# Decoder step on one core: conditioning blocks loaded ahead of x, the first 40 output tiles computed before the root, and TensorE held to program order

## The chip, the core and the metric

One core of a Trainium2 chip runs the whole program. TensorE (PE, with its weight loads PEld) multiplies into PSUM, VectorE (DVE) and ScalarE (ACT) read and write PSUM and SBUF, GpSimd (POOL) works on SBUF, and SyncE (SP) issues the DMAs. The time is that of one execution in device microseconds; several executions are made and their median is the number that counts.

## What is computed

A decoder layer for 256 prompt tokens and 8 x 4 sample tokens (288 columns in all), with model width 2048. What bears on the change is its beginning:

```python
mod = (jax.nn.silu(c) @ w_ada + b_ada).reshape(n, N_MOD, 1, D_MODEL)
sh_m, sc_m, gt_m, sh_f, sc_f, gt_f = [mod[:, i] for i in range(N_MOD)]
h = _rms(x, g_mix) * (1 + sc_m) + sh_m      # _rms: x * rsqrt(mean(x*x) + eps) * gain
proj = h @ w_in                             # 2048 -> 9216
```

After it come a gated convolution, a spatial gating, two projections, a residual, a second modulated norm, a SwiGLU layer of 5632 and a final norm. The conditioning `c` has nine rows: one for the prompt, eight for the sample groups.

## The kernel before

Everything is kept transposed: 128 features on the partitions, 288 tokens along the free axis, so `x` is 16 tiles (kt 0 to 15) of 128x288. `proj` has 72 output tiles. Every fp32 product is made of three fp32r matmuls: ACT rounds the weights to `hi` (line 331) and DVE makes `lo` = weights - `hi` (line 333), 512 columns at a time, and the activations are split in the same way; lines 344 to 346 then issue hi x hi, hi x lo, lo x hi.

Weights come in blocks of up to 1 MB through one ring of five `raw` buffers, all issued by SP in the order of a list of steps; a block is loaded five blocks ahead (`AHEAD`), when the block that had its buffer is done with. `proj` is accumulated in four passes over the input features: wA takes kt 0 for all 72 tiles (six blocks of 12 tiles) and stores each tile to `part[m]` (`sinkA`: ACT copies odd tiles, line 434, DVE even ones, line 436); wB adds kt 1 and 2 (nine blocks of eight tiles, `sinkB`, line 439), wC kt 3 to 7 (24 blocks of three), wD kt 8 to 15. Between them the conditioning blocks run on TensorE (`Ada`, line 274): aA gives the shift and scale of kt 0, aB of kt 1 and 2, aC and aD of kt 3 to 7, aE of 8 to 15. An `Ada` unit ends with `tail`: ACT copies the sums out (line 289), TensorE gathers or transposes them (293, 298), DVE adds the bias (302).

The order at the start: SP issues c, the first constants, all of x (2.4 MB), the other constants and then the four aA blocks. ACT squares x tile by tile, DVE adds the squares up, six small matmuls (167) and a power on POOL (171) give the root per token (`rstd1`), `norm1` spreads it over the partitions (177) into `rb1`, and `normed` x tiles are multiplied by it: kt 0 on DVE (197), the fifteen others on POOL (`norm1b`, 410). `mk_h1` makes the modulated activations h1 by ACT (205), POOL (208, 209), ACT (211) and DVE (216). Only then can the first wA matmul run.

The program is scheduled by a planner that orders each engine's instructions by a model of their costs; `issue_after(i)` tells it to place an instruction behind i on its engine. Each engine then works through its own queue strictly in that order, waiting on semaphores.

Of the kernel before, what the change touches and what calls it, by code (L numbers as in the profile page):

```python
# [15 lines left out]
NB = 8  # L16
# [6 lines left out]
SPB = 4  # L23
GK = 0.7978845608028654
# [21 lines left out]
    "wA": (0, 1, 12),  # L46
# [31 lines left out]
def _body(tc, nc, d, pc, pw, pslot, ptmp, pps):  # L78
# [35 lines left out]
    ident = cp[:, C_ID : C_ID + 128]  # L114
# [13 lines left out]
    V.memset(ones, 1.0)  # L128
    mhalf = const("mhalf", [P, 3])
# [70 lines left out]
    def modulate(ks, get, gm, sh0, out):  # L200
        hs, his = {}, {}

        def affine(k, t):
# [5 lines left out]
            G.tensor_tensor(sam(h[:, TP:]), sam(h[:, TP:]), bc4(mod[:, sh0 + k, 1:]), ALU.add)  # L209
# [34 lines left out]
    class Step:  # L244
        defer = False
        raw = None
        parts = None

    class Ada(Step):
# [15 lines left out]
        def run(self):  # L265
# [4 lines left out]
            for k in range(self.nk // ks):  # L270
                for j in range(4):
                    kt = self.blk * self.nk + k * ks + j % ks
                    o = (k * 4 + j) * w
                    self.last = PE.matmul(  # L274
                        acc[32 * j : 32 * j + 32, :w],
                        cs[:, kt, :],
                        self.raw[:, o : o + w],
                        start=(kt < ks),
                        stop=(kt >= 16 - ks),
                        tile_position=(0, 32 * j),  # L280
                        skip_group_check=True,
                    )
# [26 lines left out]
    class Blk(Step):  # L309
        def __init__(self, name, idx, rhs, sink):  # L310
            self.name, self.idx, self.rhs, self.sink = name, idx, rhs, sink
# [7 lines left out]
        def split(self, most=99):  # L319
# [4 lines left out]
            for s in range(len(self.parts), n, per):  # L324
# [6 lines left out]
                A.copy(hi, self.raw[:, s * 128 : e * 128])  # L331
# [5 lines left out]
        def run(self):  # L337
            for j in range(self.nm):
                ps = psmain()
                for k in range(self.nk):  # L340
# [3 lines left out]
                    PE.matmul(ps[:, :T], wh, ah, start=first, stop=False)  # L344
                    PE.matmul(ps[:, :T], wh, al, start=False, stop=False)  # L345
                    PE.matmul(ps[:, :T], wl, ah, start=False, stop=last)  # L346
                self.sink(self.idx * self.nm + j, ps)

    class KBlk(Blk):
        def run(self):  # L350
# [3 lines left out]
            for k in range(self.nk):  # L354
                ah, al = self.rhs(self.idx * self.nk + k)
                first, last = self.idx + k == 0, self.idx == nb - 1 and k == self.nk - 1
                for j in range(self.nm):
                    ps = S["kps"][j]
                    wh, wl = self.parts[k * self.nm + j]
                    PE.matmul(ps[:, :TU], wh, ah, start=first, stop=False)  # L360
                    PE.matmul(ps[:, :TU], wh, al, start=False, stop=False)
                    self.last = PE.matmul(ps[:, :TU], wl, ah, start=False, stop=last)
# [49 lines left out]
    xn = {}  # L412
    h1 = {}

    def mk_h1(k0, k1):
        def f():
            V.scalar_tensor_tensor(  # L417
                gm1[:, k0:k1, :],
                mod[:, 16 + k0 : 16 + k1, :],
                1.0,  # L420
# [430 lines left out]
```

## Time and profile before

| | us |
|---|---|
| median of three runs | 1659.89 (1659.48 to 1660.59) |
| the profiled execution, its own time | 1658.19 |
| its span on the core | 1656.2 |
| TensorE busy, share of the span | 1624.6, 98% |
| first matmul of wA starts at | 23.42 |

The profiled execution is 1.7 us under the median, and its span lies 2.0 us inside its own time. Times below count from the start of the span. A matmul's row lasts until its result has landed, so rows of matmuls overlap; their pace is read from how many start in a stretch.

### The profile page before, as it was taken

Reading aid. Unit: us, or ns where it says so; the run is one execution under the profiler, and the core shown is the slowest. Engines: PE = TensorE matmul, PEld = TensorE weight load, DVE = VectorE, ACT = ScalarE, POOL = GpSimd, SP = SyncE. Lnnn points to the kernel's source line nnn. Section 1 sums busy time; section 2 is a strip of 40 time slices with the busy share of each in tenths; the row PEclk is TensorE's granted clock in tenths of the full one; section 3 lists DMA queues with packets and bytes.
Section 4 is the critical chain, followed back from the end, with each engine's and each line's share of the span. In section 5 each row is a group of like instructions: output and inputs, shape, how many; then the busy total and the mean of one; then the engine's idle time right before and its main releaser. Section 6 shows DMA issues by size and latency. Waiting matters only on the chain.

```text
span 1656.2 us, 31141 instructions
## 1 busy us (share of the span) xinstructions
PE 1624.6 (98%) x12456; PEld 1556.0 (94%) x12456; DVE 995.4 (60%) x2034; ACT 736.2 (44%) x1371; POOL 63.9 (4%) x154
## 2 busy tenths in 40 slices
PE   5999999999999999999999999999999999999997
PEld 5889899989898999999999899999999999999997
DVE  5767556878755557557844455555555555555565
ACT  4534334643444434446733344444444444344453
POOL 3000001000000000002300000000000000000000
PEclk9999999999999999999999999999999999999998
DMA  7685786567777776674466755443454444645342
GB/s 267 254 335 207 277 313 246 191 233 261 277 308 277 282 286 251 251 263 154 152 255 254 304 170 196 171 163 137 158 206 163 168 141 156 204 161 171 126 170 76
DMA packets 56034, 357.59 MB, mean 216 GB/s; under 512 B 6369, under 2 KB 8577, under 8 KB 22737
## 3 DMA queue, kind: packets, MB, share of 16 engines
q1 hardware_dynamic: 55536, 354.88, 58.8%
q8 instruction: 97, 1.59, 0.4%
q0 software_dynamic: 352, 0.73, 0.1%
q14 instruction: 49, 0.39, 0.1%
HBM read 352.50 MB, written 3.09 MB: 215 GB/s over the span
## 4 chain that ended last, share of the span: by engine, by line
issue 50%; DVE 0%; ACT 0%; POOL 0%; PE 0%; POOLq 0%; DVEq 0%
DVE x L651 0%; PE px L177 0%; ACT t L205 0%; ACT s L211 0%; POOL t L208 0%; ACT hi L331 0%; POOL t L209 0%; POOLq L837 0%; DVE s L197 0%; DVE s L216 0%; DVEq L837 0%; POOLq L208 0%
## 5 line engine op out<-in xcount | busy, mean ns | idle before, releaser
L344 PE MATMUL pm<-s,hi 128*128 128x288 f32 x3712 | 1100.1, 297 | 7.2 <-ACT s L434 3.1
L345 PE MATMUL pm<-s,hi 128*128 128x288 f32 x3712 | 1097.1, 296 | 0.1
L346 PE MATMUL pm<-s,lo 128*128 128x288 f32 x3712 | 1094.1, 295 | 0.0
L331 ACT CAST hi<-raw 128x512 fp32r<-128x512 f32 (+1 forms) x966 | 581.9, 610 | 793.0 <-PE pm L345 661.7
L333 DVE TENSOR_TENSOR lo<-raw,hi 128x512 fp32r<-128x512 f32 (+1 forms) x966 | 652.5, 682 | 450.7 <-ACT hi L331 434.7
L344 PEld LDWEIGHTS pm<-s,hi 128*128 128x128 f32 x3712 | 698.8, 188 | 26.7 <-issue 14.6
L346 PEld LDWEIGHTS pm<-s,lo 128*128 128x128 f32 x3712 | 699.2, 188 | 0.2 <-DVE lo L333 0.2
L345 PEld LDWEIGHTS pm<-s,hi 128*128 128x128 f32 x3712 | 698.8, 188 | 0.5 <-DVE s L216 0.5
L274 PE MATMUL ada<-raw,cs 128*32 128x512 f32 (+2 forms) x960 | 91.1, 519 | 12.3 <-DMA raw<-in_aA 12.2
L439 DVE TENSOR_TENSOR s<-pm,s 128x288 f32<-128x288 f32 x144 | 64.3, 454 | 48.4 <-PE pm L346 48.2
L274 PEld LDWEIGHTS ada<-raw,cs 128*32 128x32 f32 x960 | 29.0, 113 | 56.4 <-issue 39.0
L447 DVE TENSOR_TENSOR s<-pm,s 128x288 f32<-128x288 f32 x72 | 32.8, 455 | 24.1 <-PE pm L346 23.8
L190 ACT CAST s<-t 128x288 fp32r<-128x288 f32 (+1 forms) x76 | 32.9, 432 | 21.0 <-DVE t L550 9.6
L192 DVE TENSOR_TENSOR s<-t,s 128x288 fp32r<-128x288 f32 (+1 forms) x76 | 34.8, 458 | 7.1 <-ACT s L190 7.0
L171 POOL TENSOR_TENSOR r<-r,mhalf 128x3 f32<-128x3 f32 x4 | 3.8, 957 | 908.2 <-DVE r L170 908.2
L232 DVE SCALAR_TENSOR_TENSOR x<-pm,mod,x 128x256 f32<-128x256 f32 x80 | 37.9, 474 | 0.0
L623 DVE SCALAR_TENSOR_TENSOR t<-t,pm 128x288 f32<-128x288 f32 x42 | 19.1, 454 | 25.3 <-PE pm L346 25.3
L231 DVE TENSOR_TENSOR t<-pm,mod 128x32 f32<-128x32 f32 x80 | 15.3, 191 | 29.6 <-PE pm L346 29.6
L155 DVE TENSOR_TENSOR acc<-acc,t 128x288 f32<-128x288 f32 x48 | 21.9, 456 | 12.3 <-ACT t L150 11.0
L150 ACT ACTIVATE t<-x 128x288 f32<-128x288 f32 x45 | 19.1, 442 | 21.3 <-DVE x L233 20.6
L457 ACT ACTIVATE s<-s 128x288 f32<-128x288 f32 x32 | 14.2, 445 | 14.2 <-DVE s L447 14.1
L208 POOL TENSOR_TENSOR t<-s,gm 128x32 f32<-128x32 f32 x32 | 11.3, 357 | 235.7 <-DVE gm L417 219.1
(114 smaller groups left out, 494.5 us busy)
## 6 DMA issues: line engine op xcount, KB each, us to landing
raw<-in_fi SPq DMA_DIRECT2D x84, 1024.0 KB, 4.8
raw<-in_a SPq DMA_DIRECT2D x64, 1024.0 KB, 6.4
raw<-in_f SPq DMA_DIRECT2D x64, 704.0 KB, 4.1
raw<-in_wD SPq DMA_DIRECT2D x36, 1024.0 KB, 6.3
raw<-in_wC SPq DMA_DIRECT2D x24, 960.0 KB, 6.2
raw<-in_aE SPq DMA_DIRECT2D x16, 1024.0 KB, 8.0
raw<-in_wo SPq DMA_DIRECT2D x16, 1024.0 KB, 7.2
raw<-in_wB SPq DMA_DIRECT2D x9, 1024.0 KB, 7.2
```

The source lines that it names most:

```text
L155: V.tensor_tensor(self.acc, self.acc, self.last, ALU.add)
L190: A.copy(hi, a)
L192: V.tensor_tensor(lo, a, hi.bitcast(F32), ALU.subtract)
L232: V.scalar_tensor_tensor(x[:, m, :TP], ps[:, :TP], mod[:, gt0 + m, 0:1], x[:, m, :TP], ALU.mult, ALU.add)
L274: self.last = PE.matmul(acc[32 * j : 32 * j + 32, :w], cs[:, kt, :], self.raw[:, o : o + w], start=(kt < ks), stop=(kt >= 16 - ks), tile_p ...
L331: A.copy(hi, self.raw[:, s * 128 : e * 128])
L333: V.tensor_tensor(lo, self.raw[:, s * 128 : e * 128], hi.bitcast(F32), ALU.subtract)
L344: PE.matmul(ps[:, :T], wh, ah, start=first, stop=False)
L345: PE.matmul(ps[:, :T], wh, al, start=False, stop=False)
L346: PE.matmul(ps[:, :T], wl, ah, start=False, stop=last)
L439: V.tensor_tensor(part[m], ps[:, :T], part[m], ALU.add)
L447: V.tensor_tensor(a, ps[:, :T], a, ALU.add)
```

## The change

Five things are done. **Loads:** SP issues aA block 0 first, then c, aA 1, the constants, aA 2 and 3, kt 0 of x, wA block 0, kt 1 to 5 of x; the rest of x and the other constants come behind wA blocks 1, 2 and 8. **Blocks:** wA has nine blocks of eight tiles instead of six of twelve. **Without the root:** for the first 40 tiles (`RAWX`) the kt 0 activation is x times its gain, with ten more columns that carry the shift (`scaled`); the root is made meanwhile (squares on POOL and ACT, their sum on TensorE in `sums1`), and `rescale` multiplies the stored tiles by `rb1` on POOL and adds the sample groups' shift terms. `sinkB` adds the prompt's shift. **Order:** every ada and block matmul is placed behind the one that precedes it in the list of steps (`behind(S["pe"])`), and that list is written out anew up to the end of wC. **Filling:** `warm` issues matmuls of `ones` by `ones` before and between the aA blocks.

```diff
+RAWX = 40
-    "wA": (0, 1, 12),
+    "wA": (0, 1, 8),
...
+    def warm(n, after=None):
+        ps = psmisc()
+        with behind(after):
+            for _ in range(n):
+                PE.matmul(ps[:, :P], ones, ones, start=True, stop=True)
+
+    def scaled(k, gm, columns):
+        a = tmp(TU)
+        A.activation(a[:, :TP], x[:, k, :TP], AF.Copy, scale=gm[:, k, 0:1])
+        G.tensor_tensor(sam(a[:, TP:T]), sam(x[:, k, TP:]), bc4(gm[:, k, 1:]), ALU.mult)
+        columns(a[:, T : T + NC])
+        G.memset(a[:, T + NC :], 0.0)
+        return split(a, TU)
...
-                    PE.matmul(ps[:, :T], wh, ah, start=first, stop=False)
-                    PE.matmul(ps[:, :T], wh, al, start=False, stop=False)
-                    PE.matmul(ps[:, :T], wl, ah, start=False, stop=last)
+                    with behind(S.get("pe")):
+                        PE.matmul(ps[:, : self.n], wh, ah, start=first, stop=False)
+                    PE.matmul(ps[:, : self.n], wh, al, start=False, stop=False)
+                    S["pe"] = self.last = PE.matmul(ps[:, : self.n], wl, ah, start=False, stop=last)
...
+    def squares1(k0, k1, m):
+        def f():
+            for k in range(k0, k1):
+                q = sq[k] = slot()
+                if k % 3:
+                    G.tensor_tensor(q, x[:, k, :], x[:, k, :], ALU.mult)
+                else:
+                    with behind(evA[m]):
+                        A.activation(q, x[:, k, :], AF.Square)
+        return Do(f)
+
+    def sums1():
+        ps = S["sq"] = psmisc()
         for k in range(16):
-            ss.add(x[:, k, :])
-        S["ss1"] = ss
+            j = k % 4
+            with behind(wA[2].last):
+                PE.matmul(
+                    ps[32 * j : 32 * j + 32, :T],
+                    ones[:, :32],
+                    sq.pop(k),
...
-    def norm1b():
-        for k in range(1, 16):
-            xn[k] = slot()
-            G.tensor_tensor(xn[k], x[:, k, :], S["rb1"], ALU.mult)
+    def rescale(m0, m1):
+        def f():
+            for m in range(m0, m1):
+                a = part[m]
+                with behind(S["aff"]):
+                    G.tensor_tensor(a[:, :T], a[:, :T], S["rb1"], ALU.mult)
+                G.tensor_tensor(sam(a[:, TP:T]), sam(a[:, TP:T]), bc4(a[:, T + 1 : T + NC]), ALU.add)
+        return Do(f)
...
     def sinkB(m, ps):
+        a = part[m]
+        if m < RAWX:
+            V.scalar_tensor_tensor(a[:, :T], ps[:, :T], a[:, T : T + 1], a[:, :T], ALU.add, ALU.add)
+            part[m] = a[:, :T]
+        else:
+            V.tensor_tensor(a, ps[:, :T], a, ALU.add)
...
-    steps = [Do(squares1)] + aA[:2] + [Do(rstd1)] + aA[2:] + [Do(norm1)]
-    aA[3].defer = True
-    steps += [Do(lambda: wA[0].split(1)), mk_h1(0, 1), Do(lambda: wA[0].split()), Do(norm1b)]
...
-    steps += weave(wA, visits(ada("aB"), 2, mk_h1(1, 3)), 1, 4)
-    steps += weave(wB, visits(ada("aC"), 4) + visits(ada("aD"), 2, mk_h1(3, 8)), 0, 6)
-    steps += weave(wC, visits(ada("aE"), 4, mk_h1(8, 16)), 2, 17)
+    steps = [Do(silu), Do(lambda: warm(6))]
+    for s in aA:
+        steps += [s, Do(lambda s=s: warm(2, s.last))]
+    steps += [Do(early0), Do(lambda: warm(6, aA[3].last)), wA[0]]
+    steps += [Do(lambda: setattr(wA[1], "after", evA[3])), squares1(0, 6, 3), wA[1], squares1(6, 11, 9), squares1(11, 16, 15), wA[2], Do(sums1), Do(rstd1)]
+    steps += [wA[3], Do(norm1), mk_h1(0, 1)] + aB[:2] + [wA[4], wA[5], wA[6]] + aB[2:]
+    steps += [gain(1, 3), wA[7], mk_h1(1, 3), wA[8], rescale(0, 24)]
+    steps += wB[:1] + aC[:4] + wB[1:2] + [rescale(24, RAWX)] + wB[2:3] + aC[4:] + [gain(3, 7)] + wB[3:4] + [mk_h1(3, 4)]
+    steps += wB[4:5] + aD + [gain(7, 8), mk_h1(4, 5)] + wB[5:6] + [mk_h1(5, 6)] + wB[6:7] + [mk_h1(6, 7)] + wB[7:8]
+    steps += [mk_h1(7, 8)] + wB[8:]
+    steps += weave(wC[:16], visits(aE, 4, gain(8, 16)), 2, 15)
+    for i in range(8):
+        steps += [mk_h1(8 + i, 9 + i), wC[16 + i]]
...
-    load_x()
-    for s in stream[:AHEAD]:
+    aA[0].load()
+    SY.dma_start(ct, d["c"])
+    aA[1].load()
+    SY.dma_start(cp1, d["cpack1"])
+    for s in aA[2:]:
         s.load()
+    load_x(0, 1)
+    wA[0].load()
+    load_x(1, 6)
+    pieces = {wA[1]: (6, 11), wA[2]: (11, 16)}
```

In `mk_h1` the normed tile of kt 1 to 15 is now made on DVE (line 197) when it is needed, not on POOL.

## Rows read from the trace of the kernel before

**Rows 1.** The page: span, busy time by engine, granted clock in 40 slices.
```profile
span 1656.2 us, 31141 instructions
...
PE 1624.6 (98%) x12456; PEld 1556.0 (94%) x12456; DVE 995.4 (60%) x2034; ACT 736.2 (44%) x1371; POOL 63.9 (4%) x154
...
PEclk9999999999999999999999999999999999999998
```

**Rows 2.** TensorE's waits over the whole span: total us, times, longest.
```profile
PE ada L274 <- DMA raw<-in_aA: 12.2, 1, 12.2
PE pm L344 <- ACT s L434: 3.1, 2, 2.3
PE pm L344 <- ACT s L211: 2.3, 1, 2.3
PE pm L344 <- DVE s L436: 1.5, 1, 1.5
```

**Rows 3.** Busy time by stretch, all engines: us, PE, PEld, DVE, ACT, POOL, clock, DMA.
```profile
0.00:5.00 5.00, 0.00 (x0) 0.00 (x0) 1.21 (x5) 1.61 (x2) 0.20 (x4) 1.00 0.56 169
...
10.00:15.00 5.00, 2.45 (x34) 1.54 (x34) 3.92 (x11) 2.28 (x6) 0.00 (x0) 1.00 1.03 416
...
30.00:35.00 5.00, 4.95 (x26) 4.96 (x27) 3.06 (x6) 2.19 (x5) 5.00 (x7) 0.66 0.12 48
...
23.42:37.04 13.62, 11.20 (x54) 10.09 (x54) 11.63 (x17) 6.68 (x15) 13.62 (x14) 0.87 0.41 145
37.04:44.20 7.16, 7.16 (x53) 7.16 (x54) 6.48 (x14) 5.57 (x13) 0.24 (x1) 1.00 0.57 211
```

**Rows 4.** TensorE's timeline at the start: start, us, instruction, count, wait.
```profile
12.17 2.27 PE L274 MATMUL ada<-raw,cs 128*32 128x128 f32 x32 [12.17 <-DMA raw<-in_aA]
...
17.36 1.93 PE L274 MATMUL ada<-raw,cs 128*32 128x128 f32 x32
19.22 1.65 PE L177 MATMUL px<-cp,r 128*128 128x128 f32 x6
20.66 0.45 PE L298 MATMUL px<-cp,ev 128*128 128x18 f32 x2
23.42 0.85 PE L344 MATMUL pm<-s,hi 128*128 128x288 f32 x2 [2.30 <-ACT s L211]
```

**Rows 5.** Timeline of all engines, from the last aA matmul to the first of wA.
```profile
2.60 0.32 ACT L134 ACTIVATE ctt<-ct 128x144 f32<-128x144 f32 x1 [0.58 <-DMA ct<-in_c]
...
19.36 0.27 ACT L289 COPY ev<-ada 128x128 f32<-128x128 f32 x1 [6.48 <-PE ada L274]
...
21.16 0.24 DVE L302 TENSOR_TENSOR mod<-px,cp 128x9 f32<-128x9 f32 x2 [3.53 <-PE px L298]
...
21.93 0.60 ACT L205 ACTIVATE t<-s,mod,gm 128x256 f32<-128x256 f32 x1 [0.62 <-DVE s L197]
```

**Rows 6.** Groups of TensorE instructions by line and shape: busy us, mean ns.
```profile
L344 PE MATMUL pm<-s,hi 128*128 128x288 f32 x3712 | 1100.1, 297 | 7.2 <-ACT s L434 3.1 <-ACT s L211 2.3 <-DVE s L436 1.5
...
L360 PE MATMUL pm<-s,hi 128*128 128x298 f32 x48 | 14.5, 302 | 0.0
```

**Rows 7.** Durations min/median/max ns: POOL 22 to 36 us; line 333 twice; line 439.
```profile
L410 POOL TENSOR_TENSOR s<-x,rb x15: 792/1015/1272, 22.5 to 36.0; 128x288 f32<-128x288 f32 x15
...
L333 DVE TENSOR_TENSOR lo<-raw,hi x7: 765/1278/1286, 23.1 to 35.4; 128x512 fp32r<-128x512 f32 x7
...
L333 DVE TENSOR_TENSOR lo<-raw,hi x12: 676/682/694, 37.3 to 56.9; 128x512 fp32r<-128x512 f32 x12
...
L439 DVE TENSOR_TENSOR s<-pm,s x144: 443/457/459, 67.5 to 295.5; 128x288 f32<-128x288 f32 x144
```

**Rows 8.** Timeline around the wait in wA, one aC visit, and POOL's small operations.
```profile
62.72 0.41 PE L344 MATMUL pm<-s,hi 128*128 128x288 f32 x1 [2.28 <-ACT s L434]
...
85.31 3.66 PE L274 MATMUL ada<-raw,cs 128*32 128x256 f32 x64
...
60.27 0.44 POOL L209 TENSOR_TENSOR t<-t,mod 128x32 f32<-128x32 f32 x2
```

More of the change, by code (lines that the diff above doesn't have):

```diff
@@ L1 @@
+from contextlib import ExitStack
 import numpy as np
@@ L128, in _body @@
     V.memset(ones, 1.0)
+    groups = const("groups", [P, 1])
+    G.memset(groups, 0.0)
+    for j in range(4):
+        G.memset(groups[32 * j : 32 * j + 1, :], 1.0)
     mhalf = const("mhalf", [P, 3])
@@ L245, in _body @@
         defer = False
+        after, lead = None, 0
         raw = None
@@ L273, in run @@
                     o = (k * 4 + j) * w
[L274 to L282, printed above, removed]
+                    with behind(S.get("pe")):
+                        S["pe"] = self.last = PE.matmul(
+                            acc[32 * j : 32 * j + 32, :w],
+                            cs[:, kt, :],
+                            self.raw[:, o : o + w],
+                            start=(kt < ks),
+                            stop=(kt >= 16 - ks),
+                            tile_position=(0, 32 * j),
+                            skip_group_check=True,
+                        )
             if (self.blk + 1) * self.nk == 16 and not self.defer:
@@ L359, in run @@
                     wh, wl = self.parts[k * self.nm + j]
-                    PE.matmul(ps[:, :TU], wh, ah, start=first, stop=False)
+                    with behind(S.get("pe")):
+                        PE.matmul(ps[:, :TU], wh, ah, start=first, stop=False)
                     PE.matmul(ps[:, :TU], wh, al, start=False, stop=False)
-                    self.last = PE.matmul(ps[:, :TU], wl, ah, start=False, stop=last)
+                    S["pe"] = self.last = PE.matmul(ps[:, :TU], wl, ah, start=False, stop=last)
             if self.idx == nb - 1:
@@ new lines, in sums1 @@
+    def sums1():
+        ps = S["sq"] = psmisc()
+        for k in range(16):
+            j = k % 4
[4 more added lines that the diff above has]
+                    sq.pop(k),
+                    start=(k < 4),
+                    stop=(k >= 12),
+                    tile_position=(0, 32 * j),
+                    skip_group_check=True,
+                )
+    def rstd1():
+        q = tmp()
+        A.copy(q, S["sq"][:, :T])
+        r = S["r1"] = ptmp.tile([P, 3], F32, tag="r", name=nm("r"), bufs=2)
+        ps = psmisc()
+        for c, t0 in enumerate(TB):
+            PE.matmul(ps[:, c : c + 1], q[:, t0 : t0 + P], groups, start=True, stop=True)
+        V.tensor_scalar(r, ps[:, :3], 1.0 / D, EPS, ALU.mult, ALU.add)
+        G.tensor_tensor(r, r, mhalf, ALU.pow)
@@ L413, in _body, with early0, columns @@
[L413 to L427 removed]
+    def early0():
+        gain1(0, 1)
+        def columns(t):
+            G.tensor_copy(t, mod[:, 0, :])
+            G.tensor_tensor(t[:, 1:], t[:, 1:], t[:, 0:1].to_broadcast([P, NB]), ALU.subtract)
+        xe[0] = scaled(0, gm1, columns)
+        wA[0].after, wA[0].lead = S["hi"], SEG
@@ L429, in _body @@
+    def mk_h1(k0, k1):
+        return Do(lambda: modulate(range(k0, k1), lambda k: normed(k, S["rb1"]), gm1, 0, h1))
     part = {}
     def sinkA(m, ps):
-        part[m] = slot()
+        n = TU if m < RAWX else T
+        part[m] = slot(shape=(P, n))
         if m % 2:
-            A.copy(part[m], ps[:, :T])
+            evA[m] = A.copy(part[m], ps[:, :n])
         else:
-            V.tensor_copy(part[m], ps[:, :T])
+            V.tensor_copy(part[m], ps[:, :n])
     def sinkB(m, ps):
+        a = part[m]
[4 more added lines that the diff above has]
+            V.tensor_tensor(a, ps[:, :T], a, ALU.add)
@@ L439, in sinkB, with sinkC @@
+    def sinkC(m, ps):
         V.tensor_tensor(part[m], ps[:, :T], part[m], ALU.add)
```

88 lines of the change are left out of this document (45 added, 43 removed).

## The prediction, made before the change was run

> **What bounds the kernel now.** I read the page first: TensorE is busy for 1624.6 of 1656.2 us and no other engine passes 60% [rows 1]. So only three things can shorten the run: less work for TensorE, TensorE standing still for less, or a higher clock for it. The granted clock is at its upper level in nearly every slice [rows 1], so the second view is TensorE's list of waits [rows 2]. It is short and almost all of it lies at the start: 12.2 us for the first aA block, and 2 to 3 us each behind lines 211, 434 and 436. The third view is the busy time by stretch [rows 3]. From 37.04 us TensorE runs dense: 53 matmuls in 7.16 us, 0.135 us each. From 23.42 to 37.04 it starts only 54 in 13.62 us, where 54 x 0.135 = 7.3 would do, so 6.3 us are lost there. Two causes can be read from the same rows: the clock falls (0.66 on average from 30 to 35, that is between the levels of 1.2 and 2.4 GHz, after TensorE had stood still for line 436), and DVE is busy for 11.6 of 13.6 us, because POOL works through the whole stretch on `norm1b` and line 333 takes 1278 ns instead of 682 [rows 7]. One more stop of 2.3 us follows at 62.7 [rows 8]. What can be won is thus the wait before 23.42, these 6.3, and 2.3.
>
> **The change part by part.**
>
> *The start moves forward.* Before, aA's first matmul waits until 12.17 because x lies ahead of aA in SP's queue [rows 4]. Now aA block 0 (0.52 MB), c, aA 1 and so on come first. Over the first 5 us the queues moved 169 GB/s, 0.85 MB, later 416 GB/s [rows 3]; so block 0 and c (0.6 MB) are in at about 4.3 us. From c's landing to finished activations took 0.9 to 1.0 us (2.60 plus ACT's 0.32 [rows 5] and two DVE operations of about 0.3), and the landing itself is seen some tenths later: I let aA start at 5.9. All four blocks are in by (2.3 - 0.85) / 0.416 + 5 = 8.5, before TensorE has come to the last of them. TensorE needs 1.9 us for two aA blocks [rows 4], 3.8 for four, and the `warm` matmuls between them (two of two passes each time; the nearest row is line 177, where six passes of the same shape took 1.65 us, 0.24 at most for one with its way through the array, at a cold start [rows 4], and I estimate half of that at the upper clock) add 0.45 to 0.95 three times. So aA ends at about 11.7, bounds 10.5 and 13.
>
> *From aA to the first matmul.* Before: 19.36 to 23.42, 4.1 us [rows 4, 5]; of these, line 298 stood about 0.8 behind the spreading of the root (line 177), and ACT at 21.93 waited 0.6 for the normed tile. Now the root is out of this chain, but POOL has four operations in it (0.22 us each [rows 8], about 0.8) beside ACT's 0.60, and ten more columns. I take 2.9 us: first wA matmul at 14.6, bounds 13 and 17. The gain here is 23.4 - 14.6 = 8.8 us. TensorE is kept occupied by six more `warm` matmuls, so that I expect wA to begin near the upper clock; if not, the lower one costs about what it did from 30 to 35: 26 matmuls where 37 would fit, 11 x 0.135 = 1.5 us.
>
> *What goes away behind it.* POOL's `norm1b` (15 x 1.0 us [rows 7]) no longer lies on wA; the 6.3 us and the 2.3 us (`gain` and `mk_h1` of kt 1 and 2 are now apart, with block 7 of wA between them) are to be won: 8.6.
>
> *What TensorE gets in addition.* 40 x 3 matmuls are ten columns wider: line 360 against 344 is 302 to 297 ns [rows 6], 120 x 5 ns = 0.6 us. `sums1` is 16 matmuls of two passes; an aC visit makes 64 passes of 256 columns in 3.66 us, 57 ns each [rows 8], so 32 of 288 columns take about 2.1 and the change to and fro 0.4. The root's and the spread's 12 small passes now lie inside wA: 1.4 at 0.12 each, the same estimate. Together 4.5 us. Before, such work lay in the wait, where it was free.
>
> *DVE and POOL in wA.* A block of eight tiles is 24 x 0.14 = 3.3 us of TensorE. DVE has four copies at 0.45 and two of line 333, 1.8 + 1.4 = 3.2 us undisturbed: it just keeps up. POOL's ten squares (like line 410, 0.79 to 1.27) fall on the first three blocks, and there line 333 goes to 1.28: 1.8 + 2.6 = 4.4. One block of split weights lies ready as a cushion, so of 3 x 1.1 us I count 1.5, bounds 0 and 3.5. Waits for `lo` at the first matmul and for the root's small matmuls, which stand in TensorE's queue with all of wA behind them: 1.0 (0 to 2.5).
>
> *The rescaling in wB.* This is the step that I trust least. POOL must multiply 40 stored tiles by `rb1` (a 128x288 operation with two SBUF inputs, as line 410: 0.79 alone, 1.24 to 1.27 against line 333) and add the sample terms (0.22). Alone that is 1.0 us a tile. Per block of wB four runs of line 333 fall in, each holding POOL up by 0.45: 8 x 1.0 + 4 x 0.45 = 9.8 us, 1.2 a tile, 49 us for 40. It can start when kt 1 and 2 are modulated, about as block 7 ends. From there TensorE passes wA block 8 (3.3), some 1.5 of rest, five wB blocks of 48 matmuls (32) and two aC visits (4.3 each with the change to and fro) and can be four PSUM tiles ahead (3.2): 49 us. So POOL and TensorE are level, and behind POOL's queue stand the sums of `sinkB` on DVE (with line 333 for the next blocks behind them) and, from kt 3 on, POOL's share of `mk_h1`, on which a cast on ACT waits with line 331 behind it. Line 439 itself is not lengthened (443 to 459 ns over all 144 [rows 7], one input in PSUM). DVE has 8 x 0.45 + 4 x 1.28 = 8.7 us a block against TensorE's 6.5 plus 1.7 of aC: again level. I count 3.0 us of loss, bounds 0 and 8.
>
> The Trainium skill (SBUF — State Buffer, "Who interferes with whom") says that DVE and GpSimd share a port pair as an exclusive lock, that a DVE instruction with two SBUF inputs meets it against a GpSimd instruction that reads SBUF, and that one with at most one SBUF input does not. The trace agrees: line 333 doubles to 1278 ns, line 439 stays at 457. It speaks against this change, which gives POOL 80 such reads beside DVE. By a strict lock a block would cost the sum of both, 8 x 1.0 + 4 x 0.68 = 10.7 us, and the five 54 instead of 49: 5 us lost here where I count 3, and 1654 in all. Rival 3 is the same mechanism with more collisions.
>
> *DVE's normed tiles* (15 x 0.45 us) fall in wB and wC, where DVE is at 60% on the whole: nothing. wC's own order and aE's denser visits: same work, nothing, bounds -1 and +2.
>
> **Sum.** 8.8 + 8.6 - 4.5 - 1.5 - 1.0 - 3.0 = 7.4 us less. The profiled span would go to 1648.8. Against the median, 1659.9 - 7.4 = 1652.5; I say 1652.
>
> **The rivals.**
> 1. *The clean case.* POOL keeps ahead, the cushions take the rest: 8.8 + 8.6 - 4.5 - 1 = 12 us less, about 1647.5. For it: two of the three losses are level sums. Against it: three level sums at once.
> 2. *Half of it.* The start is late (17 instead of 14.6: c waits behind a whole weight block, and TensorE begins cold) and the fixed order makes TensorE wait where the planner was wrong about the root: 2.4 + 1.5 + 1 less gain, 2 to 3 us left, 1657. For it: at 30 to 35 us a short stop already cost the clock.
> 3. *POOL sets the pace, and the kernel is slower.* If every rescaling collides, a tile costs 1.27 + 0.57 = 1.84 us (a 32-column operation that waits for a DVE operation is stretched by about 0.35), 74 us for 40 against the 49 that TensorE leaves: 25 us lost. It turns the sign when POOL needs more than about (49 + 10) / 40 = 1.5 us a tile. Half-way, at 1.6 us, the loss is 15 us and the time 1659.9 - 10.4 + 15 = 1664. For it: from 23 to 30 us POOL's rows were at 1.24 without a break. Against it: there DVE did nothing but line 333; wB has eight PSUM sums a block, which don't collide.
> 4. *The head is covered anyway*: the matmuls come earlier but find no weights, since five buffers and one queue feed them. Up to the end of wB about 33 MB come in by the sizes of the blocks, 80 us at 416 GB/s [rows 3], against some 110 us of TensorE. I give this no case of its own.
>
> **How the numbers follow.** The forecast's own case (5.5 to 11 us less) has 0.55, the clean case 0.18, half 0.16, POOL 0.11. A measurement of this kernel can tell some 0.2%, 3.3 us, from no change. Faster by more than that: 0.55 + 0.18 and a third of the half case, 0.78. Slower by more: most of POOL's case, 0.09. Within: 0.13. The range reaches from beyond the clean case, 1645.5, to the middle of the half case and a little on, 1658.5; beyond it lie POOL's case and a bit on each side, together 0.2.
>
> **What would show it.** The first wA matmul between 13 and 17 us; granted clock 1.00 from there; no stop behind 434 near 60 us; POOL busy without a break for 45 to 50 us in wB and `rescale` at about 0.8 to 1.25 us. Wrong it would be if TensorE waits in wB for DVE's sums behind POOL for more than 8 us, if a wait of ACT on POOL holds up line 331, or if the first matmul comes after 18 us.

## The result, and the profile after

| | before | after |
|---|---|---|
| median, us (lowest to highest) | 1659.42 (1659.03 to 1660.59) | 1665.75 (1664.22 to 1666.45) |
| the profiled execution, its own time | 1658.19 | 1666.33 |
| its span on the core | 1656.2 | 1664.6 |
| first wA matmul | 23.42 | 13.91 |

After to before is 1.0036, with a 95% interval of 1.0023 to 1.0049: the changed kernel is 6.3 us **slower**, where 7.4 us less were forecast. The page of after (its span, busy time, granted clock):

```profile
span 1664.6 us, 31381 instructions
...
PE 1631.9 (98%) x12522; PEld 1559.4 (94%) x12522; DVE 1011.9 (61%) x2036; ACT 736.8 (44%) x1364; POOL 104.8 (6%) x238
...
PEclk9989999999999999999999999999999999999998
```

TensorE's share is 98% in both pages [rows 1]; of what concerns TensorE only the granted clock looks different, with an 8 in its third slice (83 to 125 us). That is a hint, but it does not say how much was lost where. A second reading does: in the trace of each kernel I numbered the main matmuls (288 or 298 columns into `pm`) by their start and compared the same numbers. Number 215 is the last of wA, 640 lies just before the end of wB, and wD begins between 1500 and 2000. Each row is one profiled execution, and the last line is taken from the unrounded starts.

| n-th main matmul starts at, us | 0 | 215 | 640 | 1500 | 2000 | last PE row |
|---|---|---|---|---|---|---|
| before | 23.4 | 66.0 | 134.3 | 263.7 | 331.4 | 1646.4 |
| after | 13.9 | 59.1 | 140.7 | 270.9 | 341.3 | 1654.9 |
| after minus before | -9.5 | -7.0 | +6.3 | +7.2 | +9.9 | +8.5 |

So the start was won, 2.5 us of it were given back in wA, **13.3 us were lost between 215 and 640**, 0.9 up to 1500, 2.7 from 1500 to 2000, and 1.4 won over the rest. (These two executions lie 8.1 us apart, the medians 6.3.) The lines of after that answer to those of before follow. Lines have moved: the matmuls are 371 to 373 (before 344 to 346), the cast to `hi` is 357 (331), `lo` 359 (333), `sinkA` 500 and 502 (434, 436), `sinkB` 507 (439), `gain` 482, `rescale` 473 and 474, POOL's part of `mk_h1` 231 and 232, ACT's cast in it 234.

TensorE's timeline at the start (start, us, instruction, wait), which answers to [rows 4]:

```profile
5.53 1.08 PE L299 MATMUL ada<-raw,cs 128*32 128x128 f32 x16 [1.54 <-DVE cs L142]
...
10.62 0.64 PE L299 MATMUL ada<-raw,cs 128*32 128x128 f32 x16
...
13.91 0.40 PE L371 MATMUL pm<-s,hi 128*128 128x298 f32 x1
15.19 0.41 PE L372 MATMUL pm<-s,hi 128*128 128x298 f32 x1 [0.87 <-DVE s L198]
```

The aA blocks run from 5.53 to 11.3 instead of from 12.17 to 19.2, and the first wA matmul comes 9.5 us earlier. Its second one waits 0.87 us for DVE's `lo` of the activation, beside POOL's squares.

TensorE's list of waits (total, times, longest), which answers to [rows 2]:

```profile
PE pm L373 <- DVE lo L359: 10.1, 4, 9.5
PE pm L371 <- ACT s L500: 3.0, 3, 2.0
PE ada L299 <- DVE cs L142: 1.5, 1, 1.5
```

Before, its longest wait was the 12.2 us at the start. Now it is one of 9.5 us on a DVE `lo`. TensorE's timeline there:

```profile
88.91 0.29 PE L372 MATMUL pm<-s,hi 128*128 128x288 f32 x1
98.65 0.61 PE L373 MATMUL pm<-s,lo 128*128 128x288 f32 x1 [9.45 <-DVE lo L359]
99.05 0.45 PE L371 MATMUL pm<-s,hi 128*128 128x288 f32 x1
...
104.52 0.29 PE L373 MATMUL pm<-s,lo 128*128 128x288 f32 x1
```

TensorE stands still from 88.91 to 98.65. What DVE did meanwhile, and what POOL did:

```profile
88.62 0.43 DVE L327 TENSOR_TENSOR mod<-px,cp 128x18 f32<-128x18 f32 x4 [3.93 <-PE px L318]
88.96 8.93 DVE L482 SCALAR_TENSOR_TENSOR gm<-mod,cp 128x36 f32<-128x36 f32 x1
97.82 2.72 DVE L359 TENSOR_TENSOR lo<-raw,hi 128x512 fp32r<-128x512 f32 x4
```

```profile
88.49 0.81 POOL L473 TENSOR_TENSOR s<-s,rb 128x288 f32<-128x288 f32 x1
89.25 0.24 POOL L474 TENSOR_TENSOR s<-s 128x32 f32<-128x32 f32 x1
89.45 0.80 POOL L473 TENSOR_TENSOR s<-s,rb 128x288 f32<-128x288 f32 x1
...
97.06 0.79 POOL L473 TENSOR_TENSOR s<-s,rb 128x288 f32<-128x288 f32 x1
97.81 0.89 POOL L474 TENSOR_TENSOR s<-s 128x32 f32<-128x32 f32 x2
```

One DVE instruction of 36 elements a partition, `gain` of kt 3 to 6, lasts **8.93 us**; the other instructions of its line take 0.17 to 0.18. It begins while POOL multiplies a tile and ends when POOL's last multiplication does. Nine pairs of POOL's rescaling go by in between, at 0.95 us a pair, each row beginning about 0.05 us before the last one ends. Behind the instruction stand, on DVE, the four `lo` of the next weight block, and behind those TensorE. The small operations just ahead of it (line 327, one input in PSUM) ran beside the same POOL instruction in 0.17 to 0.18 us each.

Busy time by stretch (us, PE, PEld, DVE, ACT, POOL, granted clock, DMA share, GB/s), which answers to [rows 3]:

```profile
56.70:60.10 3.40, 3.13 (x13) 3.13 (x14) 3.27 (x7) 1.21 (x3) 3.40 (x6) 0.51 0.01 2
60.10:87.28 27.18, 26.33 (x270) 22.68 (x269) 21.52 (x33) 4.79 (x9) 27.18 (x48) 1.00 0.76 279
...
90.80:104.40 13.60, 5.75 (x24) 5.75 (x25) 11.80 (x9) 1.96 (x4) 9.12 (x19) 0.50 0.64 255
104.40:110.00 5.60, 5.60 (x44) 5.60 (x44) 4.94 (x11) 1.57 (x3) 0.00 (x0) 1.00 0.17 37
```

The stop also costs the clock: 0.50 was granted from 90.8 to 104.4, the lower level of 1.2 GHz. In it 24 matmuls start at 0.24 us apiece instead of 0.133, so 2.6 us go on top. With the stop (9.74 less the 0.13 that a matmul takes, 9.6) and the small gaps left of it (0.63 and 0.55 over the pace at 72.9 and 76.8) that is 13.4 us, against the 13.3 of the table: the loss is placed.

Two smaller ones. The stop that was to vanish from wA is there again, at 53.55, and clock 0.51 behind it (TensorE, then ACT, then POOL):

```profile
53.55 0.29 PE L373 MATMUL pm<-s,lo 128*128 128x288 f32 x1
55.84 0.40 PE L371 MATMUL pm<-s,hi 128*128 128x288 f32 x1 [2.00 <-ACT s L500]
```

```profile
52.96 1.10 ACT L228 ACTIVATE t<-s,mod,gm 128x256 f32<-128x256 f32 x2
54.02 0.95 ACT L234 CAST s<-t 128x288 fp32r<-128x288 f32 x2
54.88 0.61 ACT L357 CAST hi<-raw 128x512 fp32r<-128x512 f32 x1
55.40 0.69 ACT L500 COPY s<-pm 128x288 f32<-128x288 f32 x2
```

```profile
53.42 0.57 POOL L232 TENSOR_TENSOR t<-t,mod 128x32 f32<-128x32 f32 x1
```

ACT's copy of a PSUM tile (line 500) stands behind the modulation of kt 1 and 2 (two activations, line 228, and two casts, line 234) and a weight cast, which keep ACT busy from 52.96 to 55.50. POOL is hardly part of it: its share of kt 1 is done at 53.99, before ACT comes to the first cast, and the second cast waits 0.09 us. That is [rows 8]'s 2.28 us, 7 us earlier, and 12 matmuls at 0.24 behind it cost 1.3 more. And at the start of wD three gaps (0.66, 0.75, 1.30) stand where before had none; the first:

```profile
304.15 0.40 PE L371 MATMUL pm<-s,hi 128*128 128x288 f32 x1 [0.38 <-ACT s L234]
```

POOL's own work was cheaper than feared. Durations min/median/max, ns, from 54 to 99 us:

```profile
L473 POOL TENSOR_TENSOR s<-s,rb x40: 787/802/1250, 54.5 to 97.1; 128x288 f32<-128x288 f32 x40
...
L474 POOL TENSOR_TENSOR s<-s x40: 235/246/787, 56.2 to 98.0; 128x32 f32<-128x32 f32 x40
...
L507 DVE SCALAR_TENSOR_TENSOR s<-pm,s x24: 500/516/519, 60.7 to 84.2; 128x288 f32<-128x288 f32 x24
```

Forty tiles took 54.5 to 98.7, 44.2 us, against the 49 reckoned with: 1.1 us a tile on average, 0.95 where no DVE instruction got between. `sinkB` (line 507, one input in PSUM) was not slowed: it takes 0.52 us behind the end of POOL's queue too (101.5 and 103.0 us).

### The profile page after: what moved, and what is told of

Its sections match the earlier page's. It is cut to its first block, busy times and chain, and to the rows that moved or that the text cites. A ratio compares the mean times of both kernels' runs of the same rounds, so it can differ in the third digit from the quotient of the medians.

```text
span 1664.6 us, 31381 instructions
## 1 busy us (share of the span) xinstructions
PE 1631.9 (98%) x12522; PEld 1559.4 (94%) x12522; DVE 1011.9 (61%) x2036; ACT 736.8 (44%) x1364; POOL 104.8 (6%) x238
## 4 chain that ended last, share of the span: by engine, by line
issue 50%; DVE 0%; ACT 0%; POOL 0%; PE 0%; POOLq 0%; DVEq 0%
DVE x L720 0%; ACT t L228 0%; PE px L183 0%; ACT s L234 0%; POOL t L231 0%; ACT hi L357 0%; POOL t L232 0%; POOLq L933 0%; DVE s L239 0%; DVE s L203 0%; DVEq L933 0%; POOLq L231 0%
## 5 line engine op out<-in xcount | busy, mean ns | idle before, releaser
L371 PE MATMUL pm<-s,hi 128*128 128x288 f32 (+1 forms) x3712 | 1099.4, 296 | 6.0 <-ACT s L500 3.0
L373 PE MATMUL pm<-s,lo 128*128 128x288 f32 (+1 forms) x3712 | 1095.3, 295 | 10.1 <-DVE lo L359 10.1
L372 PE MATMUL pm<-s,hi 128*128 128x288 f32 (+1 forms) x3712 | 1097.1, 296 | 1.3 <-DVE s L198 0.9
L373 PEld LDWEIGHTS pm<-s,lo 128*128 128x128 f32 x3712 | 699.4, 188 | 11.3 <-DVE lo L359 11.3
L513 DVE TENSOR_TENSOR s<-pm,s 128x288 f32<-128x288 f32 x72 | 32.8, 456 | 36.9 <-PE pm L373 36.8
L521 DVE TENSOR_TENSOR s<-pm,s 128x288 f32<-128x288 f32 x72 | 32.8, 456 | 23.7 <-PE pm L373 23.4
L473 POOL TENSOR_TENSOR s<-s,rb 128x288 f32<-128x288 f32 x40 | 32.6, 817 | 0.0
L231 POOL TENSOR_TENSOR t<-s,gm 128x32 f32<-128x32 f32 x32 | 13.3, 416 | 230.1 <-DVE gm L482 122.7
L218 POOL TENSOR_TENSOR t<-x,gm 128x32 f32<-128x32 f32 x17 | 7.7, 452 | 295.6 <-DVE gm L657 250.4
L228 ACT ACTIVATE t<-s,mod,gm 128x256 f32<-128x256 f32 x32 | 18.6, 601 | 17.2 <-DVE s L203 9.5
```

What stands on the lines that cost most here:

```text
L371: PE.matmul(ps[:, : self.n], wh, ah, start=first, stop=False)
L372: PE.matmul(ps[:, : self.n], wh, al, start=False, stop=False)
L373: S["pe"] = self.last = PE.matmul(ps[:, : self.n], wl, ah, start=False, stop=last)
L473: G.tensor_tensor(a[:, :T], a[:, :T], S["rb1"], ALU.mult)
L513: V.tensor_tensor(part[m], ps[:, :T], part[m], ALU.add)
L521: V.tensor_tensor(a, ps[:, :T], a, ALU.add)
```

## The experiments

The theory: the loss comes from whatever has to wait for POOL's queue of rescaling **to its end** while something of TensorE's stands behind it. Rivals: the kind of instruction that `gain` is; POOL's total work; the program order on TensorE; the head. All kernels are the changed one with the edit shown. Ratios are to the kernel before, with 95% intervals.

**1. The gain off DVE.** One ACT activation per kt in place of the one DVE instruction.

```diff
-        V.scalar_tensor_tensor(gm1[:, k0:k1, :], mod[:, 16 + k0 : 16 + k1, :], 1.0, g, ALU.add, ALU.mult)
+        for k in range(k0, k1):
+            A.activation(gm1[:, k, :], mod[:, 16 + k, :], AF.Identity, bias=gmix[:, k : k + 1], scale=gmix[:, k : k + 1])
```

> Edit: the gain of kt 1 to 15 is made by ACT, one tile at a time, instead of by one DVE instruction with two SBUF inputs; nothing else is changed. Theory A (the DVE instruction of the gain of kt 3 to 6 is locked out of SBUF for as long as POOL has rescaling queued, 8.9 us, and DVE's lo casts and TensorE stand behind it): the stop of 9.7 us at 89 us goes, and with it the lower clock that follows, together 12 us: about 1653.5, faster than before. Theory B (POOL's pace is the bound, the gain only shows it): sinkB waits for rescaled tiles instead, within 3 us of 1665.7. Theory C (the gain waits for the modulation or for its tiles, not for the lock): ACT's instructions are as late as DVE's was, 1665.7.

Measured: 1666.52 us, 1.0040 [1.0027, 1.0053]: not a microsecond won. The stop at 89 us is gone, and another stands in its place. DVE, ACT and TensorE there:

```profile
89.19 5.51 DVE L359 TENSOR_TENSOR lo<-raw,hi 128x512 fp32r<-128x512 f32 x4 [0.72 <-ACT hi L357]
```

```profile
101.77 0.43 ACT L234 CAST s<-t 128x288 fp32r<-128x288 f32 x1 [8.43 <-POOL t L232]
102.11 1.13 ACT L357 CAST hi<-raw 128x512 fp32r<-128x512 f32 x2
```

```profile
97.61 0.29 PE L373 MATMUL pm<-s,lo 128*128 128x288 f32 x1
103.93 0.61 PE L371 MATMUL pm<-s,hi 128*128 128x288 f32 x1 [6.03 <-DVE s L503]
```

(Line 503 is `sinkB` in this kernel.) Without the gain in front the four `lo` take turns with POOL, 5.51 us for four. But the modulated tile of kt 3 needs two small POOL operations, and these stand in POOL's queue behind the rescaling, which ends near 101. ACT's cast waits 8.43 us for them, the weight casts behind it, and through DVE TensorE, 6.3 us and then the lower clock again. So the queue has two followers, and with the first taken away the second takes its place.

**2. Another kind of instruction.** The gain of kt 3 to 6 as a multiplication and an addition.

```diff
+            V.tensor_tensor(gm1[:, k0:k1, :], mod[:, 16 + k0 : 16 + k1, :], g, ALU.mult)
+            V.tensor_tensor(gm1[:, k0:k1, :], gm1[:, k0:k1, :], g, ALU.add)
```

> Edit: the gain of kt 3 to 6 stays on DVE with two SBUF inputs, but as two TENSOR_TENSOR instructions (times g, then plus g) in place of one SCALAR_TENSOR_TENSOR. DVE's lo casts, also TENSOR_TENSOR, got their turn between two of POOL's operations in the changed kernel (1.1 to 2.1 us). If the kind of instruction decides who gets a turn: two turns of at most 1.5 us each, stop at 89 us of 2 to 3 us, about 1656 to 1658. If any two-input DVE instruction can be locked out by a POOL queue that has no gap at that place: a stop of 8 to 9 us again, 1665.7. Theory B: 1665.7 too, with waits of sinkB.

```profile
87.79 9.93 DVE L486 TENSOR_TENSOR gm<-mod,cp 128x36 f32<-128x36 f32 x1
```

Measured: 1666.76 us, 1.0038 [1.0024, 1.0053]. The first of the two is held 9.93 us, again until POOL is done, and TensorE for 11.0. The kind of instruction is not the cause.

**3. The rescaling listed behind the gain.** Tiles 24 to 39 come after `gain(3, 7)` in the list of steps.

```diff
-... + wB[1:2] + [rescale(24, RAWX)] + wB[2:3] + aC[4:] + [gain(3, 7)] + wB[3:4]
+... + wB[1:2] + wB[2:3] + aC[4:] + [gain(3, 7), rescale(24, RAWX)] + wB[3:4]
```

> Edit: the rescaling of tiles 24 to 39 is placed behind the gain of kt 3 to 6 in the list of steps; the gain's instruction is unchanged. POOL then ends its first 24 tiles at about 80 us and is idle when the gain runs at 89. Theory A: the gain takes 0.2 us, no stop of 9.7; but POOL makes 16 tiles from 89 us at 1.0 to 1.2 us while TensorE wants one each 0.8, so 1 to 4 us of waits behind sinkB: 1654.5 to 1658. Theory B: POOL is the bound and begins later, so slower than the changed kernel by up to 8 us. Theory C: no change, 1665.7.

```profile
92.70 6.08 DVE L482 SCALAR_TENSOR_TENSOR gm<-mod,cp 128x36 f32<-128x36 f32 x1
```

Measured: 1665.72 us, 1.0033 [1.0020, 1.0045]. The experiment didn't part the two, because the list fixes an order for TensorE alone: POOL, free to go ahead, rescaled without a break from 55.4 to 99.6. The gain came later, was held 6.08 us, and TensorE stopped for 6.9. One `lo` was held too, for 4.15 us from 68.41, while three pairs of POOL passed it.

**4. Fewer tiles.** `RAWX` 32 instead of 40: eight tiles fewer to rescale, and as many that wait for the root in wA.

```diff
-RAWX = 40
+RAWX = 32
```

> Edit: 32 instead of 40 tiles without the root, so POOL's queue is 8 tiles, about 7.7 us, shorter; the gain's instruction is unchanged. Theory A: the gain's instruction ends when the queue ends, so it takes 0.5 to 1.5 us instead of 8.9 and the stop at 89 us nearly goes: 1654 to 1657. Theory B: 20% less rescaling, 1663 or so. Theory C: 1665.7.

```profile
89.12 1.38 DVE L482 SCALAR_TENSOR_TENSOR gm<-mod,cp 128x36 f32<-128x36 f32 x1
```

Measured: 1657.36 us, 0.9985 [0.9976, 0.9995]: 8.4 us less than the changed kernel for a fifth of the rescaling. POOL's queue ends at 91.3 instead of 98.7, the gain that begins at 89.12 lasts 1.38 us, and TensorE stops for 2.2. Matmul 640 starts at 130.8, 9.9 us earlier than in the changed kernel, where both had come to matmul 215 at 59 us. A loss that went with the amount of work would have fallen by a fifth of 13.3 us, 2.7; it fell by 9.8, and 3.5 are left between 215 and 640. That points at the end of the queue, but fewer tiles change the amount and the end together; experiment 5 parts them.

**5. The end of the queue behind its followers.** The last eight tiles come after the gain and after `mk_h1` of kt 3.

```diff
-... + [rescale(24, RAWX)] + wB[2:3] + aC[4:] + [gain(3, 7)] + wB[3:4] + [mk_h1(3, 4)]
+... + [rescale(24, 32)] + wB[2:3] + aC[4:] + [gain(3, 7), mk_h1(3, 4), rescale(32, RAWX)] + wB[3:4]
```

> Edit: only the order of POOL's queue. The rescaling of tiles 32 to 39 is placed behind the modulation of kt 3, which comes forward to right behind its gain; POOL's queue then ends with tile 31 at about 86.5 us, before the gain at 89, and ACT's cast of kt 3 waits for two short POOL operations instead of for eight more tiles. The gain's DVE instruction is unchanged. Theory A+B (nothing is wrong with the amount of POOL's work; what costs 12 us is what stands behind POOL's queue in order, first the gain on DVE through the lock, and when that is taken away the cast of kt 3 on ACT): both stops go, 1653 to 1655. Theory D (POOL's and DVE's shared work is too much in wB whatever the order): the wait moves to the sums of tiles 32 to 39, over 1660.

```profile
90.22 1.36 DVE L482 SCALAR_TENSOR_TENSOR gm<-mod,cp 128x36 f32<-128x36 f32 x1
```

```profile
90.73 0.79 POOL L473 TENSOR_TENSOR s<-s,rb 128x288 f32<-128x288 f32 x1
```

Measured: 1657.52 us, 0.9987 [0.9978, 0.9996]. Forty tiles again, the same work on POOL (to 104.0 us, five later than in the changed kernel), and both long stops are gone: the gain lasts 1.36 us, TensorE stops 2.1 at 90 and 1.1 and 0.7 near 97. POOL's run up to tile 31 ends at 91.5, not at the 86.5 expected, and the gain ends with it. So it is not the amount of POOL's work that makes the long stops, but what stands behind it. Not all of the loss is gone, though: from 215 to 640 this kernel takes 73.2 us against 68.3 before and 81.6 in the changed kernel, so 8.4 of the 13.3 went and 4.9 stayed. The time is 3 us above what I had thought, 1653 to 1655: the stop in wA (2.3 and its clock) and wD's start (2.7 us of gaps, then clock 0.50 for 3.4 us) are still in it.

**6. The same without the filling matmuls.** `warm` issues none.

```diff
-            for _ in range(n):
+            for _ in range(0):
                 PE.matmul(ps[:, :P], ones, ones, start=True, stop=True)
```

> Edit: e5_rescale_split without the 20 filling matmuls of ones by ones. If they only hold the clock up: aA ends 2 to 3 us earlier, wA begins at 1.2 GHz and pays 1.5 to 2 us: within 1 us of e5_rescale_split. If they are worth what they are there for, up to 3 us slower; if they only delay aA, up to 2 us faster.

Measured: 1658.33 us, 0.9992 [0.9982, 1.0001], whose interval overlaps that of experiment 5. wA begins at 13.45 and the clock is at its upper level only from 20.0. At matmul 215 the two are level (60.4 to 60.2 us): the filling buys nothing that can be measured.

**7. The same as 5 without the order.** The three edges `behind(S["pe"])` are left out; the planner places TensorE's matmuls.

```diff
-                    with behind(S.get("pe")):
+                    with ExitStack():
```

> Edit: e5_rescale_split without the edges that hold TensorE to the list's order; the planner may interleave blocks again. If the order is what keeps TensorE dense: waits of 2 to 5 us more. If the order only makes TensorE wait for the first lo: 1 us faster. I expect within 1.5 us of e5_rescale_split.

```profile
95.70 0.37 PE L371 MATMUL pm<-s,hi 128*128 128x288 f32 x1 [2.79 <-DVE s L507]
```

Measured: **1654.34 us, 0.9970 [0.9959, 0.9982]**, 5.2 us faster than the kernel before and 3.2 faster than experiment 5, where I had expected at most 1.5. The stop in wA and the gaps at wD's start are gone: matmuls 1500 to 2000 take 67.9 us, as before the change (67.6), where experiment 5 took 71.7. It has a stop of 3.4 us at 20.0 (aB's weights) and one of 3.1 at 92.6. The latter waits for a `sinkB` that stands behind four `lo`, and these took 4.96 us beside POOL, where four undisturbed take 2.7 (0.68 each [rows 7]).

**8. The modulation in wA pulled apart.** Experiment 5 with kt 1 before and kt 2 behind wA block 8.

```diff
-[gain(1, 3), wA[7], mk_h1(1, 3), wA[8], rescale(0, 24)]
+[gain(1, 3), wA[7], mk_h1(1, 2), wA[8], mk_h1(2, 3), rescale(0, 24)]
```

> Edit: e5_rescale_split with the modulation of kt 1 and 2 apart, kt 2 behind wA block 8. The stop of 2.3 us at 53.5 us, where TensorE waits for ACT's copy of a sum and ACT for POOL's share of kt 1 and 2, should fall to about 1, and with it the lower clock from 56.7 to 60 (1.6 us): 2 to 3 us faster than e5_rescale_split. If TensorE then waits for kt 2 at the start of wB instead: no difference.

Measured: 1659.38 us, 1.0003 [0.9993, 1.0013], nothing won. The stop in wA shrinks from 2.3 to 1.7, but new ones of 1.8 and 0.6 come at 57 to 60, when kt 2 is wanted.

**9. The order alone taken away.** The changed kernel with its own list, and without the edges.

```diff
-                    with behind(S.get("pe")):
+                    with ExitStack():
```

> The changed kernel with its forty tiles and its list of steps, but without the edges that hold TensorE to program order; the planner places its matmuls freely. Theory that the loss is the gain operation standing behind POOL's whole queue: the planner's costs know nothing of that wait, so the stop near 90 us stays at 6 to 10 us with 2 to 3 us of lower clock behind it, and only what the order cost by itself goes (the 2.3 us stop at 54 us and the gaps at wD's start, some 3 us in the split version): 1661.5 to 1664. Rival, that the fixed order is what makes the change slower (a free order would run other matmuls in the stop): no stop over 3 us near 90, 1652 to 1656.

DVE, ACT and TensorE:

```profile
90.06 5.00 DVE L359 TENSOR_TENSOR lo<-raw,hi 128x512 fp32r<-128x512 f32 x4
...
95.15 0.81 DVE L482 SCALAR_TENSOR_TENSOR gm<-mod,cp 128x36 f32<-128x36 f32 x1
```

```profile
105.42 0.43 ACT L234 CAST s<-t 128x288 fp32r<-128x288 f32 x1 [8.30 <-POOL t L232]
```

```profile
107.67 0.58 PE L371 MATMUL pm<-s,hi 128*128 128x288 f32 x1 [6.12 <-DVE s L507]
```

Measured: 1662.66 us, 1.0018 [1.0010, 1.0027]: still slower than before, by 2.8 us. Here the gain happens to come behind the `lo` and is through in 0.81 us. ACT's cast then waits 8.30 us for the end of POOL's queue, as in experiment 1, and TensorE 6.4. Without the program order the loss is 3.1 us smaller, and most of it stays. The 3.1 are not quite where I had placed them: in the trace wA's stop gives way to one of 3.6 us at 19.9 (aB's weights) and to one of 3.1 at 93.5 as in experiment 7, and matmul 640 comes 3.1 us later than in the changed kernel. What is won lies behind it, 2.5 us at wD's start and 2.8 spread over the rest.

**10. Both.** 32 tiles and no order.

```diff
-RAWX = 40
+RAWX = 32
...
-                    with behind(S.get("pe")):
+                    with ExitStack():
```

> Thirty-two tiles without the root instead of forty, and no program order on TensorE. If the two gains have separate places (POOL's queue is out of the way of gain, worth 8.4 us with the order kept; the order's own stops at 54 us and at wD's start, worth 3.2 us in the split version) they add up: 1654 to 1655, and matmul 1000 starts near 182 us as it did with 32 tiles and the order. Rival, that the ring of weights or DVE behind wB sets the pace by then, so that a stop avoided is lost again: 1656.5 to 1658.

Measured: 1654.15 us, 0.9965 [0.9953, 0.9977]: the medians add up as the first theory has it, to the same time as experiment 7. Where the gains lie is not shown: the profiled execution took 1658.1, 4 us over the median, and the sign named beforehand, matmul 1000 near 182 us, is not in it (186.8).

**11. Breaks in POOL's queue.** Each tile's sample terms directly behind its own multiplication, which they need, and from the 17th tile on a small memset.

```diff
-                G.tensor_tensor(sam(a[:, TP:T]), ..., ALU.add)
+                S["aff"] = G.tensor_tensor(sam(a[:, TP:T]), ..., ALU.add)
+                if m >= 16:
+                    with behind(S["aff"]):
+                        S["aff"] = G.memset(a[:, T + 1 :], 0.0)
```

> The changed kernel, but POOL's run of rescaling is broken up: each tile's sample terms come directly behind its own multiplication, and from the 17th tile on a memset of nine columns follows, which reads nothing. Theory, that the gain operation on DVE is passed over because POOL's reads follow one another without a break: it now starts within a tile, that is lasts 0.8 to 2 us instead of 8.93, and TensorE's stop at 89 us shrinks to under 3 us. POOL's queue grows longer by 0.1 to 0.2 us a tile, so it ends near 101 to 104 us, and the cast of kt 3 on ACT, which stands behind it, should stop TensorE there for 5 to 9 us as in the version with the gain on ACT: 1664 to 1669 in all. Rival, that DVE is held until POOL's queue is empty whatever stands in it: the gain lasts 10 to 14 us and the time is 1667 to 1671.

DVE, POOL, ACT and TensorE:

```profile
87.32 0.37 DVE L485 SCALAR_TENSOR_TENSOR gm<-mod,cp 128x36 f32<-128x36 f32 x1
87.61 3.19 DVE L359 TENSOR_TENSOR lo<-raw,hi 128x512 fp32r<-128x512 f32 x4
```

```profile
86.83 0.80 POOL L473 TENSOR_TENSOR s<-s,rb 128x288 f32<-128x288 f32 x1
87.71 0.68 POOL L474 TENSOR_TENSOR s<-s 128x32 f32<-128x32 f32 x1
88.45 0.11 POOL L477 MEMSET s<- 128x9 f32 x1
```

```profile
107.25 0.43 ACT L234 CAST s<-t 128x288 fp32r<-128x288 f32 x1 [18.22 <-POOL t L232]
```

```profile
109.50 0.58 PE L371 MATMUL pm<-s,hi 128*128 128x288 f32 x1 [16.30 <-DVE s L510]
```

Measured: 1674.01 us, 1.0081 [1.0064, 1.0098], 5 us above the upper end of what I expected. The gain now lasts 0.37 us instead of 8.93, and four `lo` 3.19 instead of 5 to 6. A pair now starts every 1.23 us, with breaks of 0.08 and 0.06 us around the sample terms, so the queue ends at 106.7. ACT's cast comes up early, at 89, and waits 18.22 us for its end; TensorE stands for 16.6 (line 510 is `sinkB` here). My 5 to 9 us were too little because I left the cast where experiment 1 had it.

**Where the versions stand.** The same reading as in the section on the result, as difference from the kernel before:

| n-th main matmul, us | 0 | 215 | 640 | 1500 | 2000 | 2600 | last PE row |
|---|---|---|---|---|---|---|---|
| changed kernel | -9.5 | -7.0 | +6.3 | +7.2 | +9.9 | +10.0 | +8.5 |
| experiment 4 | -10.6 | -7.1 | -3.6 | -3.9 | -1.4 | -0.6 | -0.9 |
| experiment 5 | -8.1 | -5.8 | -0.9 | -0.5 | +3.6 | +2.8 | +0.9 |
| experiment 7 | -11.0 | -4.1 | -0.2 | -0.4 | -0.2 | -0.5 | -3.2 |
| experiment 9 | -11.1 | -3.3 | +9.4 | +9.5 | +9.8 | +9.4 | +6.3 |

In experiments 7 and 9 half of an aC visit, some 1.9 us of work, has moved ahead of number 215. Two things can be read. Every version still loses between 215 and 640: 3.5 us in experiment 4 and 4.9 in 5. And experiment 7, the fastest of these, has hardly any of its start left at 640 (0.2 us) and at 2600 (0.5); the larger part of its lead in this trace comes later.

## Why the prediction was wrong

**The start: right.** First wA matmul 13.91 (14.6, bounds 13 to 17), aA from 5.53 to 11.3 (5.9 to 11.7), the upper clock in wA. The 8.8 us were 9.5 (with the same head, experiments 1 to 5 began between 12.9 and 15.3).

**Losses inside wA: half right.** At matmul 215, 7.0 us were left of the gain. The sum to that point was 8.8 + 8.6 - 4.5 - 1.5 - 1.0 = 10.4, so 3.4 are missing. The stop that the 8.6 to be won had struck out came back (2.2 over the pace), with 1.0 of lower clock before number 215, and the other waits in wA were 3.5 where 1.5 + 1.0 had been allowed. Against that, the start was 0.7 better and the added passes took 3.5 instead of 3.9. Setting `gain` and `mk_h1` apart didn't remove the stop: the copies of PSUM tiles still stand behind the four operations of the modulation on ACT.

**The rescaling in wB: the step that failed.** "I count 3.0 us of loss, bounds 0 and 8"; it was 13.3. The pace that this was worked out from was right or better: 1.1 us a tile for 1.2, 44.2 us for 40 against 49, and `sinkB` at 0.52. With the long stop avoided, 3.5 us (experiment 4) and 4.9 (5) are lost there, close to the count. The error is in what the sum left out. I balanced two throughputs and charged each meeting of DVE and POOL with one instruction's length (0.45 to 0.6 us). But the larger part of the loss, 8 to 10 us, is a latency: an instruction that has to wait for POOL's run of multiplications to end waits for all that is left of it, 8.93 us, whatever the average. The 128x36 `gain` was given no price at all there, nor the clock after such a stop (2.6). The lines to follow were in the prediction ("behind POOL's queue stand ... POOL's share of `mk_h1`, on which a cast on ACT waits with line 331 behind it"); experiments 1, 9 and 11 show that wait at 8.43, 8.30 and 18.22 us. I had not asked when POOL's queue ends against when these followers come up: 98.7 against 88.96 and about 93 (experiment 1).

**The rivals.** Rival 3 had the sign and nearly the time (1664), with the wrong mechanism: it needed 1.5 us a tile, and POOL took 1.1. Experiment 5 settles that, since POOL did the same forty tiles there and 8.4 of the 13.3 us were gone. Of rival 2 the order was real: 3.1 us (9 against the changed kernel), 3.2 (7 against 5), but in the traces it lay at wD's start and not with the root. The clean case (its sum gives 1648.0, not 1647.5) is not reached by any version. Experiments 7 and 10, at 1654.3 and 1654.2, are inside the forecast range, but not by its path: by number 640 experiment 7 has lost its start, and most of its lead comes after 2600. That they land there is in part luck.

**wC's own order, "bounds -1 and +2".** 2.7 us were lost at wD's start, outside the bounds; without the edges the stretch is back at 67.9.

**What would show it.** Of the three signs of error named, the first came about in size (9.5 us of waiting in wB), for `lo` and not for sums; the second as soon as the first was removed. Of the signs of being right, "no stop behind 434 near 60 us" failed: line 500, its successor, stopped TensorE at 53.55.

**On the page cited.** Which instructions meet is as the Trainium skill has it (SBUF — State Buffer, "Who interferes with whom"): line 327 and `sinkB`, with one input in PSUM, ran beside POOL at 0.17 and 0.52 us, while two-SBUF-input ones were held. The time that I drew from it, 1654 by the sum of both engines' work, missed for the same reason as my own.

**Left open.** Why a DVE instruction with two SBUF inputs is passed by several of POOL's in one place (8.93, 9.93, 6.08, 4.15 us) and takes turns in another (0.81; four `lo` in 5.0 to 5.5 us) with the same POOL instructions beside it. Breaks end it (experiment 11), but it also failed to occur without them (1, 9). One thing goes with it in the traces of the gain. It was held to the end of POOL's run wherever the DVE instruction ahead of it ended 0.50 to 0.57 us into one of POOL's multiplications (the changed kernel, 2, 3, and with little of the run left 4, 5 and 6). It went through as soon as the running multiplication ended where that was 0.1 to 0.3 us (7, 9, 10). Experiment 11 came up at 0.57 and went through all the same, which speaks for the breaks. For `lo` the moment does not decide: at 0.25 us one was held for 4.15 (3) and another for 1.18 (the changed kernel). No run varied the moment alone, so this is not shown as a cause. Also not traced: about 2.8 us by which experiment 7 gains on before after matmul 2600, spread thinly; the changed kernel gains 1.5 there too.

## What to carry to other kernels

When work is moved onto an idle engine, don't compare its total with the room alone: list what comes next on every queue that needs that engine or shares its path, and compare **when its queue ends** with when each of these comes up. Put the bulk behind its small, urgent followers, as experiment 5 did with eight tiles, or cut it until its end lies before them, as experiment 4. And an order written by hand for one engine fixes nothing on the others; it cost 3 us here, and taking it out while keeping the new head made a version that beats both kernels (1654.3 against 1659.5), though its trace does not put that lead down to the head.

## What was not expected of the hardware

A DVE instruction with two SBUF inputs can be passed by POOL's next instructions, not only by the one that runs: 18 of them went ahead of the gain in 8.93 us. With breaks of 0.08 and 0.06 us between POOL's rows it went through in 0.37.

The lower clock outlasts a stop by a good deal: after 9.7 us of standing, TensorE ran 24 matmuls up to 104.4 at 0.50; after 2.3 us in wA, 12 up to 60.1. A stop of as good as the same length in the kernel before (2.28 us at 62.72 [rows 8]) brought no fall: 1.00 was granted from 60 to 70 us. The three gaps at wD's start in the changed kernel (2.7 us together) brought no fall, while nearly the same three in experiment 5 did, for 3.4 us.
